# State space layer: weights split by two loads from GpSimd's queue instead of by VectorE

## The chip, the cores and the metric

The kernel runs on one core of a Trainium2 chip. The metric is the device time of one execution in microseconds, as the median of several runs. The engines are named as in the profile: PE is TensorE (PEld its weight loads), DVE is VectorE, ACT is ScalarE, POOL is GpSimd, and SP is the engine that issues the kernel's loads and stores.

## The reference

A bidirectional encoder of two layers over 512 tokens of width 1024, all in float32. Layer 0 mixes tokens by retention and neighbourhood attention, layer 1 by a state space mixer; each is followed by a feed-forward layer with a convolution. Only the state space mixer is touched:

```
def ssd_mixer(hn, w_in, conv_w, conv_b, dt_bias, a_log, d_skip, norm_g, w_out):
    proj = hn @ w_in                                   # 1024 -> 5184
    z, xbc, dt_raw = split(proj)                       # gate, x/B/C, step sizes
    xbc = silu(depthwise_conv_centered(xbc, conv_w, conv_b))
    xs, bm, cm = split(xbc)                            # 2048 values, 4 groups of B and C
    dt = softplus(dt_raw + dt_bias); log_a = -exp(a_log) * dt
    y = bidir_scan(cm, bm, xs * dt_forward, xs * dt_backward, log_a)
    y = (y + xs * d_skip) * silu(z)
    y = group_rms(y) * norm_g                          # 4 groups of 512
    return y @ w_out                                   # 2048 -> 1024
```

## The kernel before

Every product with a weight matrix is computed in three passes, so that it comes close to float32. A weight `w` is split into a high part `hi`, rounded to the reduced format float32r, and a low part `lo = w - hi`; the activations are split in the same way, and `mm3` (lines 84 to 88) issues the three matmuls hi·hi, lo·hi and hi·lo, the lines L86, L87 and L88 of the profile.

Weights come in units of 128 x 1024 floats, 512 KB. `wunit` (lines 56 to 71) fetches one: SP loads it into a staging tile `wst` (two buffers), ScalarE casts it into `whi` (three buffers), VectorE subtracts into `wlo` (three buffers); lines L81 and L82. A unit is used for 24 matmuls. Where a caller hands over its own tiles (`parts`), the split is done in two halves of 512.

The state space mixer is `mixer1` (lines 549 to 892). Its weights are 40 units of the input projection (`w_fm`, in the profile `in_c_fm`: for each of four groups B, C, four tiles of x and four of z), 16 units of the output projection (`w_out`, `in_c_out`), and one small unit for the step sizes in `steps`, which has a split of its own. For each group, the order of the work is written out by hand in `SLOTS` (line 537): projections of this group and the next (`t`, `n`), states (`s`), heads (`h`), the part between chunks (`i`), pairs (`p`), and the output of the group before (`o`). A head's decays are made from two broadcasts `pb`, loaded by SP; `ti` (L762) scales the product `pi` between chunks by a broadcast `gain`; `pair` multiplies into `py` (L778), gates with `z`, and adds the squares into `sq` on GpSimd (L788) for the group's norm (`pss`, L798).

The layer begins while the feed-forward layer before it ends: the first three units, `w0`, are loaded ahead, and their projections are done in two halves of 256 tokens, since the last tokens' norms aren't ready. The last group's output (lines 882 to 892) takes four units at once; the last two go into tiles `wo` that were states and x before.

Within the written order each engine's own queue is filled by a planner that follows dependences, buffers and priorities; `high_priority(60)` moves instructions forward in it. An engine works off its queue in order, so an instruction that waits holds up those behind it.

Of the kernel before, what the change touches and what calls it, by code (L numbers as in the profile page):

```python
# [7 lines left out]
F32 = mybir.dt.float32  # L8
R32 = mybir.dt.float32r
BF16 = mybir.dt.bfloat16  # L10
AF = mybir.ActivationFunctionType
ALU = mybir.AluOpType
# [3 lines left out]
P = 128  # L16
# [9 lines left out]
class Env:  # L26


    def __init__(self, ctx, tc):
        self.tc, self.nc = tc, tc.nc  # L30
        nc = self.nc
        pool = lambda name, bufs, **kw: ctx.enter_context(tc.tile_pool(name=name, bufs=bufs, **kw))
        self.const = pool("const", 1)
        self.res = pool("res", 1)
        self.wst = pool("wst", 2)
        self.whi = pool("whi", 3)
        self.wlo = pool("wlo", 3)
        self.gain = pool("gain", 2)
        self.tmp = pool("tmp", 7)
        self.small = pool("small", 6)  # L40
        pool("pad", 1).tile([P, 32], F32, name="pad")
        self.mm = pool("mm", 4, space=PSUM)
        self.px = pool("px", 4, space=PSUM)
        self.dram = pool("dram", 1, space=DRAM)


        head = self.const.tile([P, 96 + P], F32, name="head")
        self.ident, self.mhalf = head[:, 96:], head[:, 0:1]
        make_identity(nc, self.ident)
        nc.vector.memset(self.mhalf, -0.5)  # L50
        self.x = self.res.tile([P, NT, D], F32, name="x")
        self.xh = self.res.tile([P, KD, S], R32, name="xh")
        self.xl = self.res.tile([P, KD, S], R32, name="xl")
        self.late, self.xs = [], {}

    def wunit(self, src, parts=None):


        nc = self.nc
        st = self.wst.tile([P, 1024], F32, name="wst")  # L60
        nc.sync.dma_start(st, src)
        halves = slice(0, 512), slice(512, 1024)
        if parts is None:
            hi, lo = self.whi.tile([P, 1024], R32, name="whi"), self.wlo.tile([P, 1024], R32, name="wlo")
            with self.tc.high_priority(60):
                self.split(hi, lo, st)
            return [(hi[:, c], lo[:, c]) for c in halves]
        with self.tc.high_priority(60):
            for j, c in enumerate(halves):
                self.split(parts[j], parts[j + 2], st[:, c])  # L70
        return [(parts[j], parts[j + 2]) for j in range(2)]

    def bcast(self, row):
# [456 lines left out]
NG = 4  # L530
# [18 lines left out]
def mixer1(E, w_dt, w_fm, cw, dtc, cols, mask, w_out, g_post_row, done):  # L549
# [4 lines left out]
    nc, tc = E.nc, E.tc  # L554
    C = P
    H, H2 = SSD_H, 2 * SSD_H
    with ExitStack() as ctx:
        pool = lambda name, bufs: ctx.enter_context(tc.tile_pool(name=name, bufs=bufs))
        one, two, four = pool("m1", 1), pool("m1b", 2), pool("m1d", 4)
# [102 lines left out]
        def project(o, i, ps=None):  # L662

            g = o["g"]
            if ps is None:
                w = E.wunit(w_fm[g, i])
                ps = E.mm.tile([P, S], F32, name="mm")
                E.proj_fm(ps, w)
            if i >= 6:
                r = four.tile([P, S], F32, name="z")  # L670
                o["silu"].append((r, ps, i))
                return
            r = (one if i == 0 else two if i == 1 else four).tile(
                [P, S], F32, name="bf" if i == 0 else "cf" if i == 1 else "xf")
            wc = lambda j: cwt[:, g, i, j:j + 1]
            nc.scalar.activation(r, ps, AF.Identity, scale=wc(2), bias=wc(5))
            for j, d in ((1, 1), (3, -1), (0, 2), (4, -2)):
                a, b = (slice(d, None), slice(0, S - d)) if d > 0 else (slice(0, S + d), slice(-d, None))
                nc.vector.scalar_tensor_tensor(r[:, a], ps[:, b], wc(j), r[:, a], op0=ALU.mult, op1=ALU.add)  # L679
            o["silu"].append((r, r, i))  # L680
# [123 lines left out]
        def out_mm(o, t, ws):  # L804
            ps = E.mm.tile([P, 512], F32, name="mm")
            tt = slice(t * P, (t + 1) * P)
            for k in range(4):
                yh, yl = o["y"][k]
                E.mm3(ps, yh[:, tt], yl[:, tt], *ws[k], k == 0, k == 3)
            return ps  # L810
# [15 lines left out]
                fin(t, n, m)  # L826

        def out(o, n):
            ws = E.wunit(w_out[o["g"], n, 0]) + E.wunit(w_out[o["g"], n, 1])
            for t in range(NT):  # L830
                out_tile(o, n, t, ws)

# [3 lines left out]
                project(o, i)  # L836
            silus(o)

        w0 = [E.wunit(w_fm[0, i]) for i in range(3)]
        p0 = [E.mm.tile([P, S], F32, name="mm") for _ in range(3)]  # L840
        for c in range(2):
            for w, ps in zip(w0, p0):
# [8 lines left out]
        for g, o in enumerate(gs):  # L851
            nx = gs[g + 1] if g + 1 < NG else None
            for step in SLOTS[g].split():
                a, i = step[0], int(step[1:] or 0)
# [24 lines left out]
        def fin(t, n, m):  # L879
            E.post_half(st, t, n, m, g_post, None, four.tile([P, 512], F32, name="mg", tag="z"))  # L880

        t4 = lambda pool, tags: [pool.tile([P, 512], R32, name="wo", tag=t) for t in tags]
        xt = two.tile([P, 4, 512], R32, name="wo", tag="xt")
        ws = [E.wunit(w_out[NG - 1, 0, 0]) + E.wunit(w_out[NG - 1, 0, 1]),
              E.wunit(w_out[NG - 1, 1, 0], t4(one, ("state00", "state10", "state01", "state11"))) + E.wunit(w_out[NG - 1, 1, 1], [xt[:, i] for i in range(4)])]
        first = [out_mm(gs[-1], 0, ws[n]) for n in range(2)]
        rms(gs[-1])
        for t in range(NT):
# [148 lines left out]
```

## Time and profile before

| | |
|---|---|
| median of 3 runs | 1436.94 us (1436.8 to 1438.11) |
| profiled execution | 1439.84 us, span 1438.1 us |
| mean granted TensorE clock | 0.993 |
| PE busy | 1402.9 us (98%) |
| DVE busy | 947.7 us (66%) |
| ACT busy | 723.2 us (50%) |
| POOL busy | 62.1 us (4%) |
| DMA | 166.35 MB, all of the program's own on SP's queue |
| the state space layer | from about 620 to 1080 us |

Busy time is the time in which an engine has an instruction under way; issues of loads are not counted in it. The clock is the one that the throttle granted to TensorE, as a share of full speed; where it is below 1, the matmuls take longer. A row of the chain or of the order of time gives the start and the duration in microseconds, the engine, the line and the tiles (written <- read); in square brackets stands how long the engine was idle before it, and what ended that.

### The profile page before, as it was taken

To read this page: it belongs to the slowest core of one execution; us is meant where nothing else is said; L and a number is where in the kernel's file an instruction comes from. 1 tells how busy PE (TensorE), PEld (TensorE's weight loads), DVE (VectorE), ACT (ScalarE), POOL (GpSimd) and SP (SyncE) were. 2 spreads that over 40 slices of the span, in tenths; PEclk is the share of its full clock that TensorE was granted. 3 is DMA by queue.
4 is the path that set the end of the run, shared out by engine and by line. 5 is a ranking of instruction groups with operands and counts; after the bars stand their busy time and mean duration, and the time that the engine had idled before them with its cause. 6 is when DMAs were issued, how large, how long until landed. Compare 5 with 4: busy or idle time off the path is not lost.

```text
span 1438.1 us, 18044 instructions
## 1 busy us (share of the span) xinstructions
PE 1402.9 (98%) x6848; PEld 1145.9 (80%) x6848; DVE 947.7 (66%) x1484; ACT 723.2 (50%) x1190; POOL 62.1 (4%) x67
## 2 busy tenths in 40 slices
PE   7999999999999999999999999999889999999998
PEld 6877777888888888878777788777778888888886
DVE  7378787765655642367888796999886566564223
ACT  4356675454444431244887776577555444443221
POOL 0010110100000000000000000000110000000000
PEclk9999999999999999999999999999899999999999
DMA  7442331323333332342556354355432333323232
GB/s 254 153 140 85 94 95 53 111 95 103 88 103 102 89 103 88 103 129 89 157 184 181 96 180 141 94 151 158 147 120 76 100 93 98 103 88 103 88 103 88
DMA packets 56951, 166.35 MB, mean 116 GB/s; under 512 B 7200, under 2 KB 7968, under 8 KB 56864
## 3 DMA queue, kind: packets, MB, share of 16 engines
q1 hardware_dynamic: 56864, 165.20, 37.9%
q8 instruction: 54, 0.88, 0.3%
q14 instruction: 33, 0.27, 0.1%
HBM read 157.57 MB, written 5.51 MB: 113 GB/s over the span
## 4 chain that ended last, share of the span: by engine, by line
PE 80%; DVE 8%; ACT 4%; DMA 4%; issue 2%; POOL 1%; SPq 0%; DVEq 0%; POOLq 0%; ACTq 0%
PE mm L87 24%; PE mm L86 24%; PE mm L88 24%; DMA pb<-pd 2%; DVE wlo L82 1%; PE st L715 1%; DVE xf L679 1%; PE y L446 1%; PE pi L758 1%; PE pt L140 1%; DMA wst<-in_c_out 1%; DVE x L175 1%; DMA wst<-in_c_fm 1%; PE pt L659 1%; PE py L778 1%
## 5 line engine op out<-in xcount | busy, mean ns | idle before, releaser
L86 PE MATMUL mm<-xh,whi 128*128 128x512 f32 (+2 forms) x1216 | 464.0, 382 | 1.3 <-ACT xh L81 1.0
L87 PE MATMUL mm<-xh,wlo 128*128 128x512 f32 (+2 forms) x1216 | 463.4, 381 | 1.4 <-DVE wlo L82 1.4
L88 PE MATMUL mm<-xl,whi 128*128 128x512 f32 (+2 forms) x1216 | 463.7, 382 | 0.4 <-DVE xl L82 0.4
L82 DVE TENSOR_TENSOR wlo<-wst,whi 128x1024 fp32r<-128x1024 f32 (+1 forms) x214 | 262.9, 1230 | 222.8 <-ACT whi L81 220.0
L81 ACT CAST whi<-wst 128x1024 fp32r<-128x1024 f32 (+1 forms) x214 | 223.4, 1045 | 216.9 <-PE mm L87 154.3
L86 PEld LDWEIGHTS mm<-xh,whi 128*128 128x128 f32 (+1 forms) x1216 | 229.0, 188 | 47.1 <-ACT xh L81 2.0
L87 PEld LDWEIGHTS mm<-xh,wlo 128*128 128x128 f32 (+1 forms) x1216 | 229.0, 188 | 45.7 <-DVE wlo L82 2.7
L88 PEld LDWEIGHTS mm<-xl,whi 128*128 128x128 f32 (+1 forms) x1216 | 228.7, 188 | 44.3 <-issue 1.1
L225 DVE SCALAR_TENSOR_TENSOR cv<-mm,cwt,cv 128x511 f32<-128x511 f32 x88 | 65.7, 746 | 95.1 <-ACT cv L224 95.1
L86 PE MATMUL mm<-whi,hh 128*128 128x512 f32 x320 | 124.7, 390 | 0.0
L87 PE MATMUL mm<-whi,hl 128*128 128x512 f32 x320 | 124.6, 389 | 0.0
L88 PE MATMUL mm<-wlo,hh 128*128 128x512 f32 x320 | 124.5, 389 | 0.0
L224 ACT ACTIVATE cv<-mm,cwt 128x512 f32<-128x512 f32 x88 | 68.1, 774 | 38.7 <-PE mm L88 38.7
L81 ACT CAST hh<-cv 128x512 fp32r<-128x512 f32 x44 | 27.3, 621 | 100.1 <-DVE cv L233 99.8
L231 ACT ACTIVATE cv<-cv 128x512 f32<-128x512 f32 x44 | 27.8, 632 | 85.9 <-DVE cv L226 85.9
L86 PEld LDWEIGHTS mm<-whi,hh 128*128 128x128 f32 x320 | 60.1, 188 | 12.5
L88 PEld LDWEIGHTS mm<-wlo,hh 128*128 128x128 f32 x320 | 60.1, 188 | 12.5
L87 PEld LDWEIGHTS mm<-whi,hl 128*128 128x128 f32 x320 | 60.1, 188 | 12.3
L226 DVE SCALAR_TENSOR_TENSOR cv<-mm,cwt,cv 128x511 f32<-128x511 f32 x88 | 66.0, 750 | 3.0
L740 ACT ACTIVATE ds<-um,tok,ddt 128x128 f32<-128x128 f32 x128 | 55.7, 484 | 16.0 <-DVE e L743 15.6
L82 DVE TENSOR_TENSOR hl<-cv,hh 128x512 fp32r<-128x512 f32 x44 | 30.5, 693 | 28.9 <-ACT hh L81 28.9
L737 ACT ACTIVATE e<-pb,tok 128x128 f32<-128x128 f32 x128 | 43.0, 391 | 12.8 <-DMA pb<-pd 11.3
(236 smaller groups left out, 1891.3 us busy)
## 6 DMA issues: line engine op xcount, KB each, us to landing
wst<-in_f_up SPq DMA_DIRECT2D x88, 512.0 KB
wst<-in_f_down SPq DMA_DIRECT2D x44, 512.0 KB
wst<-in_c_fm SPq DMA_DIRECT2D x40, 512.0 KB
pb<-pd SPq DMA_DIRECT2D x64, 256.0 KB
wst<-in_ab_fm SPq DMA_DIRECT2D x20, 512.0 KB
gain<-yd SPq DMA_DIRECT2D x32, 256.0 KB
wst<-in_c_out SPq DMA_DIRECT2D x16, 512.0 KB
gain<-in_norms SPq DMA_DIRECT2D x8, 512.0 KB
```

The source lines that it names most:

```text
L81: self.nc.scalar.copy(hi, src)
L82: self.nc.vector.tensor_tensor(lo, src, hi.bitcast(F32), op=ALU.subtract)
L86: mm(out, lh, rh, start=first, stop=False)
L87: mm(out, ll, rh, start=False, stop=False)
L88: mm(out, lh, rl, start=False, stop=last)
L140: nc.tensor.transpose(pt[:, j], xs[:, j * P:(j + 1) * P], self.ident)
L224: nc.scalar.activation(o, ps, AF.Identity, scale=w(1), bias=w(3))
L225: nc.vector.scalar_tensor_tensor(o[:, 1:], ps[:, :S - 1], w(0), o[:, 1:], op0=ALU.mult, op1=ALU.add)
L226: nc.vector.scalar_tensor_tensor(o[:, :S - 1], ps[:, 1:], w(2), o[:, :S - 1], op0=ALU.mult, op1=ALU.add)
L231: nc.scalar.activation(g, g, AF.Gelu_apprx_tanh)
L737: nc.scalar.activation(e[:, c], pb[0][:, cc], AF.Identity, scale=-1.0, bias=tok[:, 0, c, h:h + 1])
L740: nc.scalar.activation(ds[:, c], um, AF.Identity, scale=ddt[:, c, h:h + 1], bias=tok[:, 1, c, H + h:H + h + 1])
```

## The change

A new function `wunit_dma` fetches a weight unit with two loads from GpSimd's queue. The first casts the weight on its way into `hi`. ScalarE writes `-hi` into `lo`. The second load reads the same weight again and adds it to `lo`, which gives `w - hi`. There is no staging tile; of every four units the fourth takes the two `wst` buffers as its `hi` and `lo`, so that four units can be in flight. The multiplication and the second load are issued with the raised priority, the first load without. All 56 units of the input and output projections in `mixer1` go through it; the two other layers, the feed-forward layers and the small unit in `steps` keep `wunit`.

```
-        self.late, self.xs = [], {}
+        self.late, self.xs, self.turns = [], {}, 0
...
+    def wunit_dma(self, src, parts=None):
+        nc = self.nc
+        halves = slice(0, 512), slice(512, 1024)
+        if parts is None:
+            self.turns = (self.turns + 1) % 4
+            hp, lp, tag = (self.wst, self.wst, "wst") if self.turns == 0 else (self.whi, self.wlo, None)
+            hi = hp.tile([P, 1024], R32, name="whi", tag=tag or "whi")
+            lo = lp.tile([P, 1024], R32, name="wlo", tag=tag or "wlo")
+            whole = [(hi, lo, src)]
+            parts = hi[:, halves[0]], hi[:, halves[1]], lo[:, halves[0]], lo[:, halves[1]]
+        else:
+            whole = [(parts[j], parts[j + 2], src[:, c]) for j, c in enumerate(halves)]
+        for hi, lo, w in whole:
+            nc.gpsimd.dma_start(hi, w)
+            with self.tc.high_priority(60):
+                nc.scalar.mul(lo, hi.bitcast(F32), -1.0)
+                nc.gpsimd.dma_start(lo, w, accum_op=ALU.add)
         return [(parts[j], parts[j + 2]) for j in range(2)]
...
-                w = E.wunit(w_fm[g, i])
+                w = E.wunit_dma(w_fm[g, i])
...
-            ws = E.wunit(w_out[o["g"], n, 0]) + E.wunit(w_out[o["g"], n, 1])
+            ws = E.wunit_dma(w_out[o["g"], n, 0]) + E.wunit_dma(w_out[o["g"], n, 1])
...
-        w0 = [E.wunit(w_fm[0, i]) for i in range(3)]
+        w0 = [E.wunit_dma(w_fm[0, i]) for i in range(3)]
...
-        ws = [E.wunit(w_out[NG - 1, 0, 0]) + E.wunit(w_out[NG - 1, 0, 1]),
-              E.wunit(w_out[NG - 1, 1, 0], t4(one, ("state00", "state10", "state01", "state11"))) + E.wunit(w_out[NG - 1, 1, 1], [xt[:, i] for i in range(4)])]
+        ws = [E.wunit_dma(w_out[NG - 1, 0, 0]) + E.wunit_dma(w_out[NG - 1, 0, 1]),
+              E.wunit_dma(w_out[NG - 1, 1, 0], t4(one, ("state00", "state10", "state01", "state11"))) + E.wunit_dma(w_out[NG - 1, 1, 1], [xt[:, i] for i in range(4)])]
```

More of the change, by code (lines that the diff above doesn't have):

```diff
@@ L70, in wunit @@
                 self.split(parts[j], parts[j + 2], st[:, c])
+        return [(parts[j], parts[j + 2]) for j in range(2)]
+    def wunit_dma(self, src, parts=None):
[15 more added lines that the diff above has]
+                nc.gpsimd.dma_start(lo, w, accum_op=ALU.add)
         return [(parts[j], parts[j + 2]) for j in range(2)]
```

## The prediction

> **What bounds the kernel now.** I read the page's busy shares and its chain first, then the busy time stage by stage, then what TensorE waits for in the state space layer, and last the order of time at the places where it waits.
>
> ```profile
> span 1438.1 us, 18044 instructions
> PE 1402.9 (98%) x6848; PEld 1145.9 (80%) x6848; DVE 947.7 (66%) x1484; ACT 723.2 (50%) x1190; POOL 62.1 (4%) x67
> PE 80%; DVE 8%; ACT 4%; DMA 4%; issue 2%; POOL 1%; SPq 0%; DVEq 0%; POOLq 0%; ACTq 0%
> ```
>
> TensorE is busy for 98% of the span and makes up 80% of the chain; VectorE, which the change relieves, makes up 8%. So a saving on VectorE is worth only what TensorE stands idle, or runs at a lowered clock, because of it. The stages, with the busy time of PE, PEld, DVE, ACT and POOL, then granted clock, DMA share and GB/s:
>
> ```profile
> 260.00:620.00 360.00, 358.49 (x1687) 300.62 (x1686) 191.81 (x240) 140.51 (x187) 4.39 (x8) 1.00 0.32 98
> 620.00:700.00 80.00, 77.27 (x428) 64.82 (x427) 60.66 (x111) 42.65 (x73) 4.39 (x8) 1.00 0.35 107
> 700.00:800.00 100.00, 96.90 (x490) 76.36 (x489) 83.79 (x156) 81.72 (x163) 4.92 (x4) 0.98 0.62 178
> 800.00:900.00 100.00, 99.92 (x520) 81.26 (x520) 78.89 (x134) 69.57 (x132) 5.75 (x4) 1.00 0.47 142
> 900.00:1000.00 100.00, 98.37 (x502) 77.24 (x501) 96.18 (x160) 67.48 (x130) 5.94 (x4) 1.00 0.46 133
> 1000.00:1080.00 80.00, 71.46 (x411) 60.09 (x409) 69.70 (x123) 45.38 (x91) 11.77 (x12) 0.91 0.45 135
> ```
>
> The layer runs from about 620 to 1080 us. Its five rows leave TensorE 80+100+100+100+80 - 443.9 = 16.1 us idle. VectorE is full there (96% in one row), ScalarE fairly full, GpSimd almost empty. Where the idle time and the lost clock lie, in rows of 10 us:
>
> ```profile
> 700.00:710.00 10.00, 9.80 (x42) 5.96 (x40) 7.32 (x12) 9.20 (x22) 0.00 (x0) 1.00 1.01 229
> ...
> 780.00:790.00 10.00, 9.11 (x53) 7.04 (x52) 8.87 (x15) 6.23 (x14) 1.27 (x1) 1.00 0.56 168
> 790.00:800.00 10.00, 10.00 (x47) 8.13 (x47) 5.09 (x16) 7.98 (x13) 1.06 (x1) 0.83 0.30 89
> ...
> 1000.00:1010.00 10.00, 10.00 (x62) 8.04 (x61) 9.30 (x22) 9.18 (x23) 0.00 (x0) 1.00 0.71 189
> ...
> 1020.00:1030.00 10.00, 6.50 (x41) 5.60 (x41) 7.34 (x14) 6.57 (x11) 0.00 (x0) 0.87 0.57 183
> 1030.00:1040.00 10.00, 9.48 (x41) 7.16 (x39) 9.82 (x16) 4.45 (x8) 3.16 (x2) 0.62 0.52 166
> ```
>
> Idle time is paid twice: 3.5 us of it at 1020 to 1030 is followed by (1-0.87)x10 + (1-0.62)x10 = 5.1 us of lost clock. And what TensorE waits for in the layer:
>
> ```profile
> PE pt L140 <- DVE xs L131: 5.7, 4, 2.9
> PE py L778 <- DVE ti L762: 3.5, 1, 3.5
> PE pss L798 <- POOL sq L788: 1.8, 2, 0.9
> PE mm L87 <- DVE wlo L82: 1.4, 2, 0.8
> ```
>
> The splits themselves (last row) hold TensorE for only 1.4 us. The first row is the normalisation at the layer's two ends, which keeps its work.
>
> **The change, part by part.** Removed from VectorE: the subtraction of every weight unit of this layer.
>
> ```profile
> L81 ACT CAST whi<-wst x60: 607/1044/1079, 624.3 to 1089.5; 128x1024 fp32r<-128x1024 f32 x59, 128x512 fp32r<-128x512 f32 x1
> L82 DVE TENSOR_TENSOR wlo<-wst,whi x59: 679/1217/2198, 625.4 to 1087.2; 128x1024 fp32r<-128x1024 f32 x58, 128x512 fp32r<-128x512 f32 x1
> L61 SPq DMA_DIRECT2D wst<-in_c_fm x40: 327/333/930, 620.6 to 993.0; - x40
> L61 SPq DMA_DIRECT2D wst<-in_c_out x16: 327/333/339, 771.2 to 1019.6; - x16
> L82 DVE TENSOR_TENSOR wo<-wst,wo x4: 684/689/693, 1022.2 to 1025.7; 128x512 fp32r<-128x512 f32 x4
> ```
>
> 40+16 = 56 units, two of them in halves: 54 x 1.22 + 4 x 0.69 = 68.6 us of VectorE. It lies beside matmuls nearly everywhere. The 56 issues of 0.33 us also leave SP's queue, where they wait for buffers ahead of the broadcasts of `pb` and `gain`; those can only start earlier, and I cost that at nothing.
>
> ScalarE: 54 casts of 1.04 us become 54 multiplications by -1 of the same size (no row shows that form at 1024 wide; the cast and, at 1.06 us in the start rows below, its neighbour bound it closely), so nothing. But each now waits for a load that was not fetched ahead.
>
> Added on GpSimd: 112 issues plus two more each for the two halved units, 116. The trace has none from this queue. Nearest rows: 0.33 us of an issue on SP, and 1.4 us, the median of the widest work GpSimd does here (`sq`, below). 116 issues are 38 to 162 us on an engine that is busy for 33 us of this layer: no bound, but a queue. I take about 1 us, between the two.
>
> Added on DMA: each weight is read twice, and the second load also reads and rewrites SBUF. The stage from 260 to 620 us moves almost only weights: 98 GB/s for a share of 0.32. Here 56 x 0.524 MB in 400 us is 73 GB/s, a share of 0.24. One more such load gives 0.47..0.62 + 0.24 = 0.71..0.86; if adding costs double, 0.95..1.10. So the upper end is a limit in the window 700 to 800, the lower is not.
>
> The new latency of a unit: load, multiply, load. Start of the layer, from the chain (start, us, what), then in order of time:
>
> ```profile
> 620.65 3.53 DMA wst<-in_c_fm
> 624.28 1.06 ACT whi L81
> ...
> 698.69 7.89 DMA pb<-pd
> ...
> 933.40 4.65 DMA wst<-in_c_fm
> ```
>
> ```profile
> 641.03 1.05 ACT L81 CAST whi<-wst 128x1024 fp32r<-128x1024 f32 x1 [0.52 <-PE mm L87]
> ...
> 642.40 1.06 ACT L81 CAST whi<-wst 128x1024 fp32r<-128x1024 f32 x1 [0.32 <-PE mm L87]
> ...
> 645.15 0.28 PE L86 MATMUL mm<-xh,whi 128*128 128x256 f32 x1
> ...
> 648.02 0.28 PE L86 MATMUL mm<-xh,whi 128*128 128x256 f32 x1
> ```
>
> A plain weight load takes 3.5 to 4.65 us. A load that adds isn't in the trace: I take 4.65 and keep 3.5 and 7.89 (the slowest load on the chain) as ends. Below 3.5 nothing speaks for it. A unit is then ready 3.6 + 1.06 + 4.65 = 9.3 us after its buffer comes free (16.8 with 7.89 twice).
>
> In steady state that is hidden. There are now four pairs of buffers (three, and both staging buffers for every fourth unit). A unit is 24 matmuls; in a dense stretch they start 0.227 us apart:
>
> ```profile
> 1021.20 0.39 PE L88 MATMUL mm<-xl,whi 128*128 128x512 f32 x1
> ...
> 1021.43 0.39 PE L86 MATMUL mm<-xh,whi 128*128 128x512 f32 x1
> ```
>
> That is 5.45 us a unit, and three others cover 16.4 us against 9.3. Behind a GpSimd instruction that waits stand the next loads, `sq` and the reciprocal roots; the loads have those 7 us, the others don't.
>
> At the start it isn't hidden. The buffers of the second and third unit come free only at 641.0 and 642.4 (the two casts, released by matmuls). Second unit: load until 644.6, multiplied at 645.7, added at 650.35. TensorE wants its low half with the unit's second matmul, at 648.1: a stall of 2.3 us (1.2 with 3.5, 5.5 with 7.89). The third is wanted 2.9 us after that and its loads run 1.4 us behind, so it adds nothing. **Start: +2.3.**
>
> The pair sums: `sq` stands in GpSimd's queue between the new loads. It ended last at `pss` twice (1.8 us).
>
> ```profile
> L788 POOL TENSOR_TENSOR sq<-sq x12: 1269/1394/2142, 746.7 to 1040.4; 128x512 f32<-128x512 f32 x12
> ```
>
> One issue ahead of it delays it by up to 1 us; in each of these two places I take a third. **Sums: +0.7** (0 to +2).
>
> The end of the last group, where TensorE waited 3.5 us:
>
> ```profile
> 1023.87 1.14 ACT L81 CAST wo<-wst 128x512 fp32r<-128x512 f32 x2 [1.15 <-DMA wst<-in_c_out]
> ...
> 1024.52 1.90 DVE L82 TENSOR_TENSOR wo<-wst,wo 128x512 fp32r<-128x512 f32 x3 [1.60 <-ACT wo L81]
> ...
> 1026.95 0.69 DVE L782 TENSOR_TENSOR y<-y,z 128x512 f32<-128x512 f32 x1 [0.53 <-ACT z L685]
> ...
> 1027.56 0.55 DVE L762 TENSOR_TENSOR ti<-pi,gain 128x384 f32<-128x384 f32 x1
> ...
> 1028.26 3.68 PE L778 MATMUL py<-e,xt 128*64 128x128 f32 x32 [3.50 <-DVE ti L762]
> ```
>
> `ti` stands behind 1.9 us of weight subtractions. Without them, and with ScalarE's `z` no longer behind a cast that waits for a load, I take 2.0 us (0 to 3.5); what is late next is `z`. Of the 5.1 us of lost clock I take half, 2.5 (0 to 5.1). The last weights have until 1032, when the products of `wo` begin. **End: -4.5.**
>
> The middle: the three rows from 700 to 1000 leave 300 - 295.2 = 4.8 us idle, and the clock loses 1.7 us at 790 (0.83). VectorE is late in some of it (`state`, `ti`), ScalarE's table loads in the rest. I take a third. **Middle: -2.2** (0 to -6.5).
>
> Sum: 2.3 + 0.7 - 4.5 - 2.2 = -3.7 us. The profiled execution took 1439.84 us for its span of 1438.1, 2.9 us above the median of 1436.94; the terms carry over to the median: **1433.2 us**. From no change a measurement here tells about 0.2%, 2.9 us.
>
> The Trainium skill, "TensorE: Matmul & The Clock Gate", section "HAM oscillation — how this bites in real kernels": a gap of more than some 3.4 us halves the clock. The trace agrees at 1020 to 1040 but not at 790 (0.9 us idle before, 1.7 us lost), so by the rule the stall at the start costs no clock, by that row 1.7 us more and the sum is -2.0.
>
> The Trainium skill, "Collectives: The Full Stack", section "The bandwidth ceiling: the fold count and why AG ≠ RS ≠ AR": an add in the DMA needs two source reads and halves the rate. No run here shows it yet; by it the streaming part of the adding load doubles, the stall at the start nears its upper end, and the sum would be about -0.5.
>
> **The rivals.** *Nothing to measure* (0.21): the stall at the start and the sums eat the gain, since TensorE was full before. For it: PE's 98%. Against it: 5.1 us of clock at one place. 1436.5 us.
>
> *ScalarE stands at the head of its queue* (0.22), the slower end: before, a cast found its load in the staging buffer; now each of 54 multiplications waits for a load just issued. Whatever stands behind on ScalarE (`e`, convolutions, `z`) waits too. Where ScalarE has room it costs nothing, but in 9 of the 35 rows of 10 us between 690 and 1040 it is over 91% busy (first 9.20 at 700, last 9.18 at 1000). A unit comes every 400/56 = 7.1 us, so 13 units fall there; at 1.2 us each that is 15 us, less the 3.7: +11.3, 1448 us. It decides from a mean wait of 0.3 us a unit in those rows. Against it: the order of the queue is planned with the loads in it.
>
> *The loads aren't hidden* (0.14): if both take 7.9 us and GpSimd issues late, a unit takes over 16.4 us. At 20 us each of 56 units lacks (20-16.4)/4 = 0.9 us: +50, less the gain, 1484 us; at 18 us +22, 1456. It decides at 16.4 us. For it: DMA share 0.95 or more at 700 to 800. Against it: the layer's other matmuls stretch a unit to 7.1 us, so the cover is mostly longer. The Trainium skill, "SBUF — State Buffer", section "Who interferes with whom": descriptors for this queue are written through a port shared with VectorE, which can hold them up; the spread of `sq` (1269 to 2142 ns, same shape) agrees that something holds GpSimd at times.
>
> **How the numbers follow.** Forecast 0.43 (1428 to 1434), wash 0.21, slower 0.36. All gains at their ends and a small stall (-3.5-5.1-6.5+1.2) would be 1423; I put 0.08 below 1428. Above 1454 lies most of the hidden-load rival, 0.11. So the range is 1428 to 1454; the forecast's own is 1428 to 1434. Faster 0.43, same 0.21, slower 0.36.
>
> **What would show it.** Right: VectorE 69 us less busy; `py` waiting under 2 us near 1025; clock above 0.8 at 1030 to 1040; a stall of 1 to 5 us for the low half near 648; no other wait of the matmuls for a GpSimd load. Wrong: ScalarE idle before the multiplications for more than 20 us in all; matmuls waiting for loads in dense stretches; DMA share near 1; adding loads over 8 us; or the planner putting the stages in another order, so that the waits named here aren't comparable.

## The result, and the profile after

The kernel after takes **1549.4 us** (1547.4 to 1551.1), against 1437.5 us (1436.8 to 1438.9) for the kernel before in the same comparison: a ratio of 1.0772, with an interval of 1.0759 to 1.0784. The change costs 112 us. The profiled execution that is shown here has a span of 1545.6 us; the lines of the code stand 21 further down than before (L86 to L88 are now L107 to L109, L82 is L103), and the new ones are L88 (casting load), L90 (multiplication) and L91 (adding load).

From the page of the kernel after, the span, the busy shares, the two big queues (packets, MB, share of 16 engines' span), the chain, VectorE's remaining splits, and the landing times of the new loads in us:

```profile
span 1545.6 us, 18106 instructions
PE 1428.7 (92%) x6848; PEld 1163.5 (75%) x6848; DVE 889.8 (58%) x1426; ACT 724.2 (47%) x1190; POOL 143.0 (9%) x183
...
q1 hardware_dynamic: 48800, 135.83, 28.7%
q0 software_dynamic: 16704, 58.73, 16.8%
...
PE 66%; issue 14%; DMA 9%; ACT 4%; DVE 4%; POOL 3%; POOLq 0%; DVEq 0%; SPq 0%; ACTq 0%
...
L103 DVE TENSOR_TENSOR wlo<-wst,whi 128x1024 fp32r<-128x1024 f32 x160 | 196.2, 1227 | 208.9 <-ACT whi L102 206.6
...
whi<-in_c_fm POOLq DMA_DIRECT2D x40, 512.0 KB, 6.5
wlo<-in_c_fm POOLq DMA_DIRECT2D x40, 512.0 KB, 6.0
```

TensorE's share of the chain has fallen from 80% to 66%, and DMA's has risen from 4% to 9%. The largest growth is in `issue`, from 2% to 14%: most of it is time in which GpSimd's queue stands behind a load that it has just issued, and the profile doesn't show what ended it. Where the time went is read from the stages. The first row of each pair is the layer and the second is what follows it, first before and then after (columns as in the prediction's stages):

```profile
620.00:1080.00 460.00, 443.92 (x2344) 359.77 (x2342) 389.21 (x681) 306.81 (x585) 32.77 (x32) 0.98 0.48 141
1080.00:1439.00 359.00, 350.99 (x1602) 292.48 (x1600) 179.89 (x220) 130.27 (x172) 2.17 (x4) 0.99 0.31 94
```

```profile
620.00:1190.00 570.00, 473.34 (x2373) 381.09 (x2373) 334.81 (x627) 309.86 (x589) 113.43 (x148) 0.92 0.68 166
1190.00:1546.00 356.00, 347.34 (x1572) 288.97 (x1570) 176.99 (x215) 128.26 (x168) 2.16 (x4) 0.99 0.30 94
```

The layer has grown from 460 to 570 us, and nothing else has: up to 620 us TensorE is busy for 608.0 us with the same 2906 matmuls in both. Of the 110 us, TensorE is idle for 570 - 473.3 = 96.7 us in place of 460 - 443.9 = 16.1, which is 80.6 us; the other 29.4 us are longer busy time at a granted clock of 0.92 in place of 0.98. (Some 30 matmuls more fall into the layer's row than before, and as many fewer into the row behind it, so a little of this is the same work in another row: over the whole span busy time grew by 1428.7 - 1402.9 = 25.8 us.) DMA share in the layer went from 0.48 to 0.68.

What the engines wait for there (engine and line, what released them, us in total, times, longest), GpSimd first, then ScalarE, then TensorE:

```profile
POOL wlo L91 <- ACT wlo L90: 252.7, 44, 12.1
```

```profile
ACT wlo L90 <- DMA whi<-in_c_fm: 85.1, 26, 8.0
ACT wlo L90 <- DMA whi<-in_c_out: 42.2, 10, 8.3
```

```profile
PE pss L819 <- POOL sq L809: 15.6, 3, 11.3
PE pt L680 <- ACT bf L709: 12.1, 2, 9.9
PE mm L107 <- ACT z L706: 9.3, 1, 9.3
PE mm L108 <- DMA wlo<-in_c_fm: 7.9, 4, 4.1
```

GpSimd stands for 253 us in front of an adding load, waiting for the multiplication; ScalarE stands for 127 us in front of that multiplication, waiting for the casting load. TensorE itself seldom waits for a weight (last row). It meets the delay mostly in what stood behind on the two queues: of its 96.7 us of idle time in the layer, 39.6 were ended by an instruction of ScalarE (1.9 before), 22.0 by VectorE (12.1), 15.6 by GpSimd's sums (1.8), and 13.5 by the landing of a weight (none). In order of time on GpSimd, with its idle time before each instruction:

```profile
773.02 0.85 POOL L91 DMA_DIRECT2D wlo<-in_c_fm  x1 [7.39 <-ACT wlo L90]
773.56 0.87 POOL L88 DMA_DIRECT2D whi<-in_c_fm  x1
781.23 0.85 POOL L91 DMA_DIRECT2D wlo<-in_c_fm  x1 [6.80 <-ACT wlo L90]
781.78 0.87 POOL L88 DMA_DIRECT2D whi<-in_c_fm  x1
790.98 0.85 POOL L91 DMA_DIRECT2D wlo<-in_c_fm  x1 [8.33 <-ACT wlo L90]
791.53 0.86 POOL L88 DMA_DIRECT2D whi<-in_c_fm  x1
```

This is the new pace: an adding load, the next unit's casting load behind it, then 7 to 8 us of standing until that one has landed and been multiplied, and only then the next pair. One unit takes 8.2 and 9.8 us here, against the 7.1 us at which the layer wants them. The queue, counted through, shows it throughout: of the 54 whole units, 37 adding loads are issued with no casting load ahead of them but their own. That order is planned, so a buffer that comes free early doesn't change it.

### The profile page after: what moved, and what is told of

It reads as the page before. It is cut to its first block, busy times and chain, and to the rows that moved or that the text cites. A ratio compares the mean times of both kernels' runs of the same rounds, so it can differ in the third digit from the quotient of the medians.

```text
span 1545.6 us, 18106 instructions
## 1 busy us (share of the span) xinstructions
PE 1428.7 (92%) x6848; PEld 1163.5 (75%) x6848; DVE 889.8 (58%) x1426; ACT 724.2 (47%) x1190; POOL 143.0 (9%) x183
## 3 DMA queue, kind: packets, MB, share of 16 engines
q0 software_dynamic: 16704, 58.73, 16.8%
## 4 chain that ended last, share of the span: by engine, by line
PE 66%; issue 14%; DMA 9%; ACT 4%; DVE 4%; POOL 3%; POOLq 0%; DVEq 0%; SPq 0%; ACTq 0%
PE mm L107 20%; PE mm L109 20%; PE mm L108 20%; DMA whi<-in_c_fm 5%; DMA whi<-in_c_out 1%; POOL wlo L91 1%; DMA pb<-pd 1%; ACT wlo L90 1%; PE y L467 1%; POOL whi L88 1%; PE pt L161 1%; DVE x L196 1%; DMA wlo<-in_c_out 0%; DMA wo<-in_c_out 0%; ACT junk L140 0%
## 5 line engine op out<-in xcount | busy, mean ns | idle before, releaser
L107 PE MATMUL mm<-xh,whi 128*128 128x512 f32 (+2 forms) x1216 | 470.9, 387 | 16.0 <-ACT z L706 9.3
L108 PE MATMUL mm<-xh,wlo 128*128 128x512 f32 (+2 forms) x1216 | 468.7, 386 | 7.9 <-DMA wlo<-in_c_fm 7.9
L109 PE MATMUL mm<-xl,whi 128*128 128x512 f32 (+2 forms) x1216 | 468.4, 386 | 0.0
L103 DVE TENSOR_TENSOR wlo<-wst,whi 128x1024 fp32r<-128x1024 f32 x160 | 196.2, 1227 | 208.9 <-ACT whi L102 206.6
L107 PEld LDWEIGHTS mm<-xh,whi 128*128 128x128 f32 (+1 forms) x1216 | 233.1, 192 | 63.1 <-ACT z L706 9.5
L108 PEld LDWEIGHTS mm<-xh,wlo 128*128 128x128 f32 (+1 forms) x1216 | 233.1, 192 | 53.3 <-DMA wlo<-in_c_fm 9.8
L109 PEld LDWEIGHTS mm<-xl,whi 128*128 128x128 f32 (+1 forms) x1216 | 232.5, 191 | 45.0 <-issue 0.7
L102 ACT CAST whi<-wst 128x1024 fp32r<-128x1024 f32 x160 | 167.2, 1046 | 196.2 <-PE mm L108 150.9
L107 PE MATMUL mm<-whi,hh 128*128 128x512 f32 x320 | 124.7, 390 | 0.0
L109 PE MATMUL mm<-wlo,hh 128*128 128x512 f32 x320 | 124.5, 389 | 0.0
L90 ACT ACTIVATE wlo<-whi 128x1024 fp32r<-128x1024 f32 x54 | 57.0, 1058 | 137.7 <-DMA whi<-in_c_fm 85.1
L759 DVE SCALAR_TENSOR_TENSOR e<-pb,tok,e 128x128 f32<-128x128 f32 x128 | 40.7, 353 | 63.4 <-DMA pb<-pd 41.6
L108 PEld LDWEIGHTS mm<-whi,hl 128*128 128x128 f32 x320 | 60.1, 188 | 12.5
L109 PEld LDWEIGHTS mm<-wlo,hh 128*128 128x128 f32 x320 | 60.1, 188 | 12.5
L107 PEld LDWEIGHTS mm<-whi,hh 128*128 128x128 f32 x320 | 60.1, 188 | 12.3
L88 POOL DMA_DIRECT2D whi<-in_c_fm x40 | 29.1, 741 | 379.4 <-PE mm L109 359.9
```

The source lines that it names most:

```text
L88: nc.gpsimd.dma_start(hi, w)
L90: nc.scalar.mul(lo, hi.bitcast(F32), -1.0)
L102: self.nc.scalar.copy(hi, src)
L103: self.nc.vector.tensor_tensor(lo, src, hi.bitcast(F32), op=ALU.subtract)
L107: mm(out, lh, rh, start=first, stop=False)
L108: mm(out, ll, rh, start=False, stop=False)
```

## The experiments

Two theories stood against each other at first. *Queue* (Q): the order landing, multiplication, adding load, next casting load in one queue lets one unit be under way. *Price* (T): the adding load itself, or the transfers, are dear, wherever they stand. A third (A) is that ScalarE, waiting for a casting load, holds up what stands behind it in its own queue. The order in which each engine does its work is planned, and an edit can change it; where two kernels have the same order on every engine, the text says so, and where it doesn't, part of a difference can come from the order. Times of the kernel before in the comparisons lay at 1437.5 to 1439.7 us, and the ratios are to those. The cuts of code are shortened to what matters.

**One unit ahead.** The next unit's casting load is issued before this unit's adding load:

```
 while len(ready) < i + 2: first_load()        # casting loads, one unit ahead
 nc.scalar.mul(lo, hi, -1.0)
 with issue_after(casting load of unit i + 1):
     nc.gpsimd.dma_start(lo, w, accum_op=add)
```

> The casting load of the next unit is put ahead of the adding load of this unit in GpSimd's queue; everything else as in the changed kernel. Theory Q (the queue: an adding load that waits for ScalarE's multiplication keeps the next casting load from being issued, so one unit is under way at a time and a unit costs landing 6.5 + multiplication 1.1 + issue 0.9, some 8.5 to 10 us): two units overlap, the time falls to 1440 to 1470 us and the period of a unit in dense stretches to about 6 us. Theory T (the transfers themselves: bandwidth, two reads of each weight): the order changes little, 1530 to 1560 us. Theory A (ScalarE standing at the head of its queue for the load): ScalarE still waits for each casting load, 1500 us or more.

Measured: 1523.5 us, 1.0596 (1.0565 to 1.0627). The order was worth 26 us of 112; the larger part is elsewhere, though not all of it as the price theory had it. Theory A's bound of 1500 us holds here, and ScalarE does still wait 53.9 + 21.4 = 75 us for casting loads, in place of 127.

**Without the addition.** The second load overwrites:

```
-    nc.gpsimd.dma_start(lo, w, accum_op=ALU.add)
+    nc.gpsimd.dma_start(lo, w)
```

> The multiplication stays and the second load still waits for it, but it overwrites the low part instead of adding to it (the low part then holds the weight). Theory Q: the waits are the same, 1530 to 1555 us. A theory that adding makes the second load slow (reading and rewriting SBUF): it lands in about the time of the casting load or less, the time falls below 1500 us.

Measured: 1482.9 us, 1.0314 (1.0258 to 1.0369). Each engine has exactly the order of the kernel after, so 66 us are due to the adding and nothing else. From its page:

```profile
q0 software_dynamic: 16704, 58.73, 13.2%
...
whi<-in_c_fm POOLq DMA_DIRECT2D x40, 512.0 KB, 4.9
wlo<-in_c_fm POOLq DMA_DIRECT2D x40, 512.0 KB, 4.0
```

Same packets, same bytes, but GpSimd's queue holds the DMA engines for 13.2% of a span of 1477.9 us in place of 16.8% of 1545.6. And not only the second load lands earlier (4.0 in place of 6.0 us): the casting load, which is the same instruction in both, does too, 4.9 in place of 6.5.

**Two casting loads that wait for nothing.**

```
-    nc.scalar.mul(lo, hi.bitcast(F32), -1.0)
-    nc.gpsimd.dma_start(lo, w, accum_op=ALU.add)
+    nc.gpsimd.dma_start(lo, w)
```

> The multiplication and the addition are left out: both loads are casting loads of the same weight, neither waits for ScalarE, so the low part holds the weight instead of the rest. Same issues, same queue, same reads from HBM. Theory Q and theory A: nothing waits in GpSimd's or ScalarE's queue for a landing, 1437 to 1455 us. Theory T: the two reads of each weight are still made, 1520 us or more. A theory that the adding itself is slow also expects a fall here, and is told apart by the next run.

Measured: 1456.3 us, 1.0129 (1.0099 to 1.0158). Reading each weight twice, with nothing that waits, costs 19 us of the 112, little more than the 16 of the next run.

**The loads of before, from GpSimd's queue.**

```
-    nc.sync.dma_start(st, src)
+    nc.gpsimd.dma_start(st, src)       # the layer's units; casts and subtractions as before
```

> The kernel before, with this layer's plain weight loads issued from GpSimd's queue into the staging tiles instead of SP's; casts and subtractions on ScalarE and VectorE as before. It measures what a load from this queue costs without cast or addition. Theory Q: a landing of 4 to 5 us with nothing that waits in the queue but the staging buffers, 1437 to 1445 us. Theory T in the form that every load from this queue lands late: landing 6 us or more and 1450 us or more.

Measured: 1453.7 us, 1.011 (1.0081 to 1.014). The loads land after 4.0 us, not late, and yet it costs some 16 us. The order differs from that of the kernel before on every engine, so whether the queue or the order makes these 16 us isn't shown.

**Adding without waiting.** The fourth corner: the addition stays, the wait for the landing goes.

```
-    nc.scalar.mul(lo, hi.bitcast(F32), -1.0)
+    nc.scalar.mul(lo, constant tile, -1.0)
```

> As the kernel after, but ScalarE's multiplication reads a constant tile instead of the high part, so the adding load no longer waits for the casting load of its unit (left out: the low part comes out as weight minus a constant). Same loads, same bytes, same ScalarE instructions as after. Chain theory (the loss is the order landing, multiplication, adding load, all in one queue): the adding load is issued right behind the casting load, so the time falls to that of the kernel with two plain casting loads or a little over it, 1456 to 1485 us. Price theory (the adding load itself is dear to the DMA engines, wait or no wait): the 66 us between the kernel without adding and the kernel after stay, 1456 + 66 = about 1520 us. If both are needed together, it is below 1485 us too, and the difference to 1456 us is what adding costs without the wait.

Measured: 1484.6 us, 1.031 (1.0282 to 1.0339). So, in us:

| | multiplication waits for the casting load | it doesn't |
|---|---|---|
| second load adds | 1549.4 | 1484.6 |
| second load overwrites | 1482.9 | 1456.3 |

Neither theory alone: the wait costs 27 us without the addition and 65 with it, the addition 28 us without the wait and 66 with it. (Only the two kernels of the first column have the same order on every engine, and the lower right one has no multiplication at all.) Each makes the other dearer: the addition lengthens landings, and the wait puts landings on the path. From the page of this run: both landings are longer still than in the kernel after, and yet it is 65 us faster. Below the page's rows stand two waits of this run: GpSimd still stands in front of the adding loads until ScalarE's queue comes to the multiplication, but for 117 us in place of 253, and ScalarE waits longer for the broadcasts `pb` from SP's queue (42.1 us; 22.7 in the kernel after, 11.3 before):

```profile
whi<-in_c_fm POOLq DMA_DIRECT2D x40, 512.0 KB, 7.2
wlo<-in_c_fm POOLq DMA_DIRECT2D x40, 512.0 KB, 8.0
```

```profile
POOL wlo L93 <- ACT wlo L92: 117.2, 43, 13.5
ACT e L760 <- DMA pb<-pd: 42.1, 12, 6.8
```

**Only the adding load on GpSimd.** Staging load from SP and cast on ScalarE as before:

```
+    nc.sync.dma_start(st, src)
-    nc.gpsimd.dma_start(hi, w)
+    nc.scalar.copy(hi, st)
     nc.scalar.mul(lo, hi.bitcast(F32), -1.0)
     nc.gpsimd.dma_start(lo, w, accum_op=ALU.add)
```

> The weight is loaded once from SP's queue into the staging tile and ScalarE casts it to the high part, as in the kernel before; ScalarE multiplies it into the low part by -1 and only the adding load goes from GpSimd's queue. VectorE has nothing to subtract in the layer. Queue theory (casting loads stuck behind waiting adding loads are the loss): nothing that opens a unit stands behind a waiting load any more, 1440 to 1465 us. Price theory (the adding load is slow on the DMA engines and its landing of about 6 us is on the way of each unit, with three units' buffers in place of four): 1480 to 1530 us.

Measured: 1522.8 us, 1.0576 (1.0545 to 1.0606). No casting load is left to be blocked, and it is still 83 us over the kernel before. (The fourth set of buffers is gone here as well.) ScalarE hardly waits for a load now, so theory A can't be the loss in this kernel: TensorE waits for the adding loads themselves, 54 us in all.

```profile
PE mm L107 <- DMA wlo<-in_c_fm: 36.5, 10, 8.5
PE mm L108 <- DMA wlo<-in_c_out: 13.6, 6, 4.6
PE mm L108 <- DMA wo<-in_c_out: 4.1, 1, 4.1
```

From the page of this kernel, and then from that of the plain loads from the same queue, the price of the adding load:

```profile
q0 software_dynamic: 8352, 29.36, 10.9%
...
wlo<-in_c_fm POOLq DMA_DIRECT2D x40, 512.0 KB, 8.1
```

```profile
q0 software_dynamic: 8064, 29.36, 6.3%
...
wst<-in_c_fm POOLq DMA_DIRECT2D x40, 512.0 KB, 4.0
```

The same 29.36 MB: adding, 10.9% x 16 x 1520.2 / 56 = 47.3 us of one DMA engine's time for a load of 512 KB; plain, 6.3% x 16 x 1451.6 / 56 = 26.1. That is 1.8 times as much. By the Trainium skill, "Collectives: The Full Stack", section "The bandwidth ceiling: the fold count and why AG ≠ RS ≠ AR", the adding step of a collective needs two source reads per chunk where a copy needs one, and comes out at about half the rate; the 1.8 measured here, for a load and not for a collective, is close to that.

**The same, adding from SBUF.**

```
-    nc.gpsimd.dma_start(lo, w, accum_op=ALU.add)
+    nc.gpsimd.dma_start(lo, st, accum_op=ALU.add)
```

> As the kernel with only the adding load on GpSimd's queue, but the adding load takes the weight from the staging tile in SBUF and not from HBM. If the second read of HBM is what makes the adding load land late, it is 10 us or more faster than that kernel; if the reading and writing back of the low part is, it is within 10 us of it or slower (the staging tile is then held longer).

Measured: 1504.2 us, 1.0447 (1.0396 to 1.0497); the load lands in 5.4 us in place of 8.1. But its time on the engines hardly falls: 10.5% x 16 x 1498.1 / 56 = 44.9 us in place of 47.3:

```profile
q0 software_dynamic: 8352, 29.36, 10.5%
...
wlo<-wst POOLq DMA_DIRECT2D x54, 512.0 KB, 5.4
```

So without the second read of HBM the load lands earlier and the kernel is 19 us faster, more than the 10 that were asked for (its two executions are 9 us apart), but the read isn't what makes the load dear.

**The multiplication twice.**

```
+    nc.scalar.mul(lo, hi.bitcast(F32), -1.0)
     nc.scalar.mul(lo, hi.bitcast(F32), -1.0)
```

> The kernel after, with ScalarE's multiplication of each unit given twice in a row, 1.06 us more between the landing of the casting load and the adding load; the same output. Serial theory (one unit is under way at a time, and what lies between its casting load and its adding load sets the pace of the layer): 56 x 1.06 = 59 us more, all or nearly all of it, 1595 to 1615 us. Rival (the pace is set by what the DMA engines can carry, and waits hide behind each other): ScalarE, 47% busy, takes it in, 1549 to 1565 us.

Measured: 1518.6 us, 1.0547 (1.0517 to 1.0578): 31 us *faster* than the kernel after, which neither theory allowed. The planned order had changed with it: 12 of 54 adding loads now have no further casting load ahead of them, where it was 37. With the casting load put one unit ahead by hand, as in the first experiment, and again the multiplication twice:

> The kernel with the next unit's casting load ahead of this unit's adding load (1523.5 us), with ScalarE's multiplication given twice; the order of the loads in GpSimd's queue is fixed by hand in both. If ScalarE's 1.06 us between the loads sets the pace: up to 59 us more, 1560 to 1585 us. If it doesn't, and the run with the multiplication given twice was faster by the planner's other order of the loads alone: 1515 to 1535 us.

Measured: 1514.8 us, 1.0531 (1.05 to 1.0561), 9 us under the first experiment with its one multiplication. So ScalarE's time between the loads does not set the pace, and the order of the loads would account for most of the 31 us. Why the doubled instruction still gains 9 us is open: the order isn't quite the same, on GpSimd's queue (49 adding loads with one casting load ahead in place of 51) or on the other engines.

**Two units ahead.** As the first experiment, with `i + 3`:

> Two units' casting loads ahead of an adding load instead of one. If it is still the order of the loads that costs, it gains again as the first step did, by 10 to 26 us: 1497 to 1513 us. If the rate at which the DMA engines get through casting and adding loads is the limit by now (their share was 0.74 in the layer with one unit ahead, up to 0.87), it stays within 10 us of 1523.5 us.

Measured: 1571.5 us, 1.0925 (1.0884 to 1.0967), slower than any order before, and outside both expectations. GpSimd in order of time says why:

```profile
773.59 0.54 POOL L93 DMA_DIRECT2D whi<-in_c_fm  x1 [2.81 <-PE mm L125]
774.12 0.91 POOL L107 DMA_DIRECT2D wlo<-in_c_fm  x1
786.43 0.54 POOL L93 DMA_DIRECT2D whi<-in_c_fm  x1 [11.40 <-PE mm L125]
786.96 0.91 POOL L107 DMA_DIRECT2D wlo<-in_c_fm  x1
```

The casting load of the unit two ahead needs a set of buffers that TensorE is still reading, and waits 11.40 us for it; the adding load of the nearer unit, ready since its multiplication ended some 10 us earlier, stands behind. The same in what TensorE waits for:

```profile
PE mm L124 <- DMA wlo<-in_c_fm: 57.0, 21, 7.2
```

One queue in order is wrong both ways: too shallow, and a casting load stands behind a wait for a landing; too deep, and an adding load stands behind a wait for a buffer.

**One unit ahead, without the addition.**

> One unit ahead, and the second load overwrites instead of adding (left out: the addition; the low part holds the weight). With the planner's order, leaving out the adding took 66 us (1549 to 1483). If the adding load costs by its time on the DMA engines whatever the order is, it takes 50 us or more here too: 1455 to 1475 us. If it costs only where the next casting load stands behind it, 25 us or less: 1498 us or more.

Measured: 1476.5 us, 1.0265 (1.0217 to 1.0312). The order is again that of its partner on every engine; the addition costs 47 us here. The expectation of 50 or more is missed by a little, the rival's 25 by much.

**Three sets of buffers in place of four.**

```
-    hp, lp = (wst, wst) if turns == 0 else (whi, wlo)
+    hp, lp = whi, wlo
```

> The kernel after without its fourth set of buffers: every unit goes into the three of the high and low part, none into the staging tiles. Serial theory (the order in GpSimd's queue lets one unit be under way, however many buffers are free): a set less costs little, 1549 to 1575 us. Rival (the units' latency against the buffers' cover, as the prediction reckoned): the cover falls from three products to two, by 5.45 us a unit, and up to that is lost in each of 56 units, 1600 us and more.

Measured: 1567.5 us, 1.0887 (1.0856 to 1.0919). A set less costs 18 us, 6% of what would be lost if the fourth set had covered a whole product per unit (56 x 5.45 = 305 us): the queue doesn't let the fourth set work.

**GpSimd's sums of squares on VectorE**, in the kernel after and in the one with plain loads from GpSimd's queue:

```
-    nc.gpsimd.tensor_tensor(o["sq"], o["sq"], sq, op=ALU.add)
+    nc.vector.tensor_tensor(o["sq"], o["sq"], sq, op=ALU.add)
```

> The kernel after, with the 12 sums of squares of the layer on VectorE instead of GpSimd, so that no load stands behind a sum that waits, and no sum behind a waiting load. If GpSimd's own work in the same queue as the loads is a large part of the loss, 15 to 40 us faster, 1510 to 1535 us; if the order of the loads alone makes it, within 10 us of 1549.

> The kernel before, its plain loads of the layer issued from GpSimd's queue (1454 us, 16 us over the kernel before), and the 12 sums of squares on VectorE. If those 16 us are the sums and the loads standing behind each other in one queue, it comes back to 1437 to 1443 us; if they are the queue's own slowness, it stays at 1450 to 1456 us.

Measured: 1546.2 us, 1.0739 (1.0708 to 1.077), and 1453.8 us, 1.0097 (1.0068 to 1.0126). Both stay where they were: the 15.6 us that TensorE waits for `sq` are a symptom, and the 16 us of the plain loads are not the sums. What they are stays open; by the expectation it would be the queue's own slowness, but the changed order isn't ruled out.

**Every fourth unit by two loads**, the others as before:

```
+    turns = (turns + 1) % 4
+    if parts is not None or turns: return wunit(src, parts)
```

> Every fourth unit of the layer (13 or 14 of 56) goes by the two loads from GpSimd's queue, the others are staged from SP's queue and split by ScalarE and VectorE as in the kernel before. If each unit by two loads has its price of 112 / 56 = 2.0 us, this is 1437 + 27 = about 1464 us. If the loss comes only from units that follow each other in GpSimd's queue, the units between give the two loads their time: 1432 to 1446 us.

> Every fourth unit by two loads as in the run of 1477 us, but the second load overwrites instead of adding (left out: the addition, in those units). A unit by two loads took there 4.9 landing + 1.06 multiplication + 5.6 landing + about 1.4 of issue = 13 us, and the two other buffers cover 2 x 5.45 = 10.9 us. Without adding the second landing is about 4.0 and the whole 11.4 us, 0.5 us over the cover: if latency against cover is the price, 13 x 0.5 = 7 us over the kernel before, 1440 to 1455 us. If the planner's order with two sorts of units is the price, it stays at 1465 us or more.

Measured: 1477.1 us, 1.0262 (1.0229 to 1.0294), and without the addition 1462.4 us, 1.0167 (1.0137 to 1.0196), in the same order. These units aren't neighbours in the queue, and yet each of the 13 costs (1477.1 - 1439.7) / 13 = 2.9 us, more than the 2.0 that was called linear. Without the addition it is (1462.4 - 1438.5) / 13 = 1.8 us, above the range for latency against cover and below that for the order. The reckoning behind that range counted the issues twice, since a landing is counted from the start of its issue: without the 1.4 us of issue a unit takes 11.6 us with the addition and 10.0 without, and the second is less than the cover of 10.9. So the addition's 1.1 us a unit (a second landing of 5.6 in place of 3.9 us) is near the 0.7 that latency against cover gives, but the 1.8 us that stay without it are not explained; the order here differs from that of the kernel before.

**Time on the DMA engines, without any addition.** The last question: is the price the DMA time of adding, or something of adding itself? The overwriting load is made dear in another way, its rows of 4 KB cut into pieces; the order stays that of the kernels after and without the addition:

```
-    nc.gpsimd.dma_start(lo, w)
+    nc.gpsimd.dma_start(lo in pieces of 128, w[:, :128] repeated)      # or 256
```

> The kernel without adding (1483 us), its overwriting load cut into pieces of 512 B (eight of the same columns in place of a row of 4 KB, so the low part holds the first columns over and over; left out: the addition and the right weight). Bytes and order stay. If the price of adding is the time that its packets hold the DMA engines, this load is dear in the same way: with the share of GpSimd's queue at 16 to 18% of the span as in the kernel after (16.8%; 13.2% without adding), the time is 1525 to 1565 us. If the price is of adding itself, the time stays at 1483 to 1500 us however high the share.

> The same with pieces of 1 KB: a smaller dose. If time on the DMA engines is the price, the time lies between 1483 us and that with pieces of 512 B, in proportion to the share of GpSimd's queue between 13.2% and that kernel's; if it is of adding itself, 1483 to 1490 us.

Measured: 1593.9 us, 1.1079 (1.1047 to 1.1111), and 1541.9 us, 1.0717 (1.0686 to 1.0748). From the page with pieces of 512 B, then of 1 KB:

```profile
q0 software_dynamic: 66624, 58.73, 16.9%
...
whi<-in_c_fm POOLq DMA_DIRECT2D x40, 512.0 KB, 8.3
wlo<-in_c_fm POOLq DMA_DIRECT2D x40, 512.0 KB, 7.7
```

```profile
q0 software_dynamic: 37952, 58.73, 15.0%
...
whi<-in_c_fm POOLq DMA_DIRECT2D x40, 512.0 KB, 6.4
wlo<-in_c_fm POOLq DMA_DIRECT2D x40, 512.0 KB, 5.8
```

No addition, and the whole loss is back. With pieces of 1 KB the time is near what the share gives in proportion, 1483 + 111 x 1.8 / 3.7 = 1537 us; with pieces of 512 B it is 29 us above the range of 1525 to 1565 that stood for this share. So adding isn't dear in a way of its own, but the share isn't the measure of the price. It orders the four kernels of the same order, while the two landings together come nearer to its size:

| | share of GpSimd's queue | casting + second landing, us | time, us | per us of landing |
|---|---|---|---|---|
| overwriting, 4 KB | 13.2% | 4.9 + 4.0 = 8.9 | 1482.9 | |
| overwriting, 1 KB | 15.0% | 6.4 + 5.8 = 12.2 | 1541.9 | 17.9 |
| adding (the change) | 16.8% | 6.5 + 6.0 = 12.5 | 1549.4 | 18.5 |
| overwriting, 512 B | 16.9% | 8.3 + 7.7 = 16.0 | 1593.9 | 15.6 |

The last column is the time above the first row over the landing above the first row: 59.0 / 3.3, 66.5 / 3.6, 111.0 / 7.1. Each us that a unit's loads land later costs the layer 16 to 19 us, as if nearly a third of the 56 units passed it on. With one unit ahead it is 47.1 us for landings of 6.2 + 7.7 against 4.9 + 4.8, 11 us for each.

One thing grows along with the landings and isn't separated from them: the time that GpSimd takes to issue the second load. On average it is 537 ns in the first row of the table, 755 in the second, 872 in the third and 895 in the fourth. From the kernels with pieces of 512 B and of 1 KB:

```profile
L93 POOL DMA_DIRECT2D wlo<-in_c_fm x40 | 35.8, 895 | 260.4 <-ACT wlo L90 242.4 <-ACT e L760 17.8
```

```profile
L93 POOL DMA_DIRECT2D wlo<-in_c_fm x40 | 30.2, 755 | 209.1 <-ACT wlo L90 192.2 <-ACT e L760 16.6 <-issue 0.2
```

With the issue of the casting load (543, 560, 741 and 565 ns) a unit's two issues grow by 0.24, 0.53 and 0.38 us over the first row. Even if all 56 units passed every bit of that on, it would be 13 us of 59, 30 of 66 and 21 of 111: a part, but the smaller one.

## Why the prediction was wrong

**The step that failed** is "In steady state that is hidden." It counted four sets of buffers as four units under way, and set a cover of 16.4 us against a latency of 9.3. Both sides were off. The cover: the queue has the multiplication's wait in it, and 37 of 54 units run with nothing ahead, so that the fourth set does little (18 us when it is taken away). The prediction did name what stands behind a waiting instruction on GpSimd, and then let the loads have "those 7 us". The latency: 6.5 + 1.06 + 6.0 is 13.6 us. That is still less than 16.4, so by the prediction's own reckoning the longer landings would have been hidden; it is the cover that wasn't there. What the step put at nothing is most of the 112 us: 66 us go when the second load overwrites, 65 when the multiplication doesn't wait for the landing, and 93 when the second load neither adds nor waits.

**The size of the loads.** It took 4.65 us for an adding load with ends of 3.5 and 7.89; the median of 6.0 lies inside. The casting load was put at 3.6 and landed in 6.5, and nothing there allowed that one load would slow the other. The shares of 0.71 to 0.86, or 0.95 and more "if adding costs double", were worked out and then enter no term of the sum. Adding does cost nearly double (1.8), and the first thing that it makes late is the next casting load.

**The rivals.** *The loads aren't hidden* had the right place, and too small a price: it kept the cover at 16.4 us, which the measured 13.6 don't pass, asked for 20 us a unit to reach 1484 us, and had no term for the queue's order. *ScalarE stands at the head of its queue* happened too, with 127 us of waiting in front of the multiplication where it reckoned with 15, and on the path that it named: 39.6 of TensorE's 96.7 us of idle time were ended by ScalarE. But more ScalarE time between the loads cost nothing, and with ScalarE hardly waiting for a load (the adding load alone on GpSimd) 83 us stayed, so it is a way in which late landings reach TensorE, and not their cause. How much would be left if only ScalarE's wait went, and GpSimd's stayed, no run shows. *Nothing to measure* fell with the forecast, since both rested on the same cover.

**What held.** VectorE's saving, 68.6 us forecast, is there: its whole splits are 160 with 196.2 us in place of 214 with 262.9, and the four halves of 0.69 are gone, 69 us in all. (The engine's busy time fell by 57.9 us only: all its durations sum to 1026.9 us before and 957.7 after, but they overlap in places, and busy time counts those once.) The start: TensorE waited 3.25 us for the low half at 652 us, forecast 2.3 with ends of 1.2 and 5.5. It cost clock too, which the sum put at nothing: 0.91 from 640 to 660 us in place of 1.00, which is 0.09 x 20 = 1.8 us, close to the 1.7 of the row at 790. The rest of the sum can't be compared, as the order of the layer changed: the sums were put at 0.7 us (0 to 2), and TensorE waited 15.6 us for them, by the same delay. Clock lost to idle time was named as "paid twice", and beside the idle time busy time did grow, by 25.8 us over the whole span.

**What the runs leave open**: the 16 us of the plain loads from GpSimd's queue, the last 1.8 us a unit of every fourth unit without the addition, the 9 us gained by a second multiplication, and how the 66 us of the addition divide between later landings and longer issues on GpSimd. No version here came under the kernel before; the nearest that splits any unit by two loads is every fourth, at 1477.1 us.

## What to carry to other kernels

Buffers are not units under way: in an in-order queue, write the issues down one behind the other, mark which of them wait for a landing, and count how many first loads have been issued at each wait; that number, not the number of buffers, is the cover. When a DMA takes over an engine's arithmetic, ask how much later it lands and how much later it makes the loads beside it land (here 2.0 and 1.6 us), and charge both to each unit that something waits for. The time for which its packets hold the DMA engines told the direction here, not the size. Before moving work off an engine that is full, ask whether the chain passes through it: VectorE had 8% of the chain here, and no run turned the 69 us saved on it into time.

## What the runs showed of the hardware

- An adding load of 512 KB holds the DMA engines 1.8 times as long as a plain one (47.3 against 26.1 us of one engine), from HBM or, at 44.9, from SBUF; a casting load hardly more than a plain one: the two casting loads that wait for nothing come to 12.8% x 16 x 1455.1 / 112 = 26.6 us each.
- The issue of the adding load is dearer too. Two groups of GpSimd in the layer, the first of the kernel after, the second of the one that overwrites (mean ns behind the busy us):

```profile
L91 POOL DMA_DIRECT2D wlo<-in_c_fm x40 | 34.9, 872 | 221.1 <-ACT wlo L90 194.9 <-ACT e L758 18.3 <-issue 7.7
```

```profile
L91 POOL DMA_DIRECT2D wlo<-in_c_fm x40 | 21.5, 537 | 173.8 <-ACT wlo L90 158.2 <-ACT e L758 15.5
```

- Pieces of 512 B in place of 4 KB, at the same bytes, made a load land in 7.7 us in place of 4.0, and the 4 KB load in front of the next in 8.3 in place of 4.9.
